# Moving the low halves of some weight blocks from VectorE to GpSimd, and splitting every u block of the selection stage

## The chip, the cores and the metric

The kernel runs on one core of a Trainium2 chip. The metric is the device time in microseconds (us) of one launch. Before the change three runs gave 1626.18, 1627.36 and 1630.89 us, median 1627.36 us.

## The reference, cut to what matters

The reference is a two-layer decoder trunk on 272 tokens (16 meta tokens and 256 sequence tokens) of width 1024, all in float32. Each layer has a token mixing part (projections, a gated recurrence, attention) and a PEER part, which is a retrieval over 16384 one-neuron experts:

```
q = (h @ wq)                      # 8 heads, two halves of 128
s = einsum(q, subkeys)            # 128 scores per half
top 16 of each half, 16 best of their 256 sums -> experts, gates (softmax)
act = gelu(h . u[expert])         # one number per token and expert
out = sum over experts of gate * act * v[expert]
```

The result is added to `h`. Both layers read 16384 x 1024 float32 numbers of `u` and as many of `v`.

## The kernel before, in words

For most tokens (208 of 256) the kernel does not gather experts. It multiplies the normalised tokens with all of `u`, in 128 blocks of 128 experts, applies gelu, multiplies with a dense matrix of gates that is zero where an expert was not selected, and multiplies with all of `v`. The other 48 tokens (and the 16 meta tokens in the first layer) take a sparse way: their rows of `u` and `v` are gathered by indirect DMAs that GpSimd issues, and VectorE does the sums.

A float32 weight block of 128 x 1024 is loaded by a DMA of SyncE into a buffer (`raw`, seven of them; later also free parts of `act` and `gtab`). To multiply at float16 speed with enough precision it is split in two float16 halves in `conv` (lines 221 to 240): ScalarE writes `hi`, the block times 1024 rounded to float16 (line 238), and VectorE writes `lo`, the block times 1024 minus `hi` (line 239). TensorE then does 24 matmuls for a block in `mm3` (lines 259 to 268): eight chunks of `hi` with the high part and with the low part of the tokens (lines 264 and 265), and then eight chunks of `lo` with the high part (line 268). There are three buffers of `hi` and three of `lo` (`NHL`), and a block is split two blocks ahead of the one that TensorE is about to multiply.

The table `WHOLE` names pairs of blocks that are not split. TensorE multiplies those in float32, with eight matmuls for a block that the records show as 16 (line 1148 for `u`, 1191 for `v`), and ScalarE and VectorE do nothing for them. In the first layer the pairs 1, 5, 9, 13 and 17 of `u` (blocks 2, 3, 10, 11, and so on up to 35) are whole, in the second layer the pairs 1, 3, 6, 10 and 14 (blocks 2, 3, 6, 7, 12, 13, 20, 21, 28, 29).

The selection runs beside this. In the query stage TensorE multiplies 16 blocks of `wq` (lines 1117 to 1131). From each head's scores VectorE takes the top 16 (`topk16`, lines 785 to 792). Then `select_idx` (lines 794 to 842) forms the experts and gates for 128 tokens at a time. In it ScalarE makes a widened copy (line 820) that needs a cast by VectorE (line 805), and an exponential (line 834), which needs a table load before it and another before the next gelu. This work is cut in steps by a generator. After each `wq` and each `u` block `pump` lets the next steps be issued until a budget is used up (line 1162: about 1.15 for a u block, plus 1.6 for an unsplit one). So the table of numbers sets how much selection work stands between two blocks in the program; a scheduler then orders the instructions of each engine, and the splitting has raised priority. All engines work in order: an instruction that waits holds up all that stands behind it on its engine.

When the second half of the tokens is selected, 24 small DMAs on GpSimd's queue (line 950) rearrange the experts and gates of the sparse tokens. After that, in steps of eight tokens, one-hot matrices are built and multiplied to the dense gates (lines 982 to 1010), up to about block 110. The gathers of the sparse tokens begin at block 56 (first layer) or 54.

Of the kernel before, what the change touches and what calls it, by code (L numbers as in the profile page):

```python
# [15 lines left out]
AF = mybir.ActivationFunctionType  # L16
ALU = mybir.AluOpType
# [29 lines left out]
WS = 1024.0  # L47
# [2 lines left out]
UB = (((56, 126, 28),), ((54, 127, 20),))  # L50
PF = 7
XV = 6
WHOLE = {"uT": ((1, 5, 9, 13, 17), (1, 3, 6, 10, 14)), "v": ((15, 24, 33, 42, 51, 60), ())}
NHL = 3
ATT = ((3, 7), (1, 7))
LRU_AT = (1, 2, 3, 4)
LRU_FIRST = 0
# [2 lines left out]
VEND = 127.0  # L60
NWARM = 48
NC2 = 112


def whole(w, l, b):
# [84 lines left out]
def trunk(tc, a, out, dbg=None):  # L150
    nc = tc.nc
    V, A, P, G = nc.vector, nc.scalar, nc.tensor, nc.gpsimd
# [13 lines left out]
    with ExitStack() as ctx:  # L166
# [15 lines left out]
        order = []  # L182
# [38 lines left out]
        def conv(n):  # L221
            while st["conv"] < min(n, len(order)):
                k = st["conv"]
                issue(len(order))
                f = raws.pop(k)
                r = f[2]
                st["conv"] += 1
                if whole(*order[k]):
                    hls[k] = (k,) + f[1:]
                    continue  # L230
                free.append((k,) + f[1:])
                if order[k][0] == "gather":
                    hook["step"](r, *order[k][2])
                    continue
                hi = hl_p.tile([128, D], F16, name="hi", tag="hi")
                lo = hl_p.tile([128, D], F16, name="lo", tag="lo")
                with tc.high_priority(offset=PRI):
                    A.activation(hi, r, AF.Copy, scale=WS)  # L238
                    V.scalar_tensor_tensor(out=lo, in0=r, scalar=WS, in1=hi, op0=ALU.mult, op1=ALU.subtract)  # L239
                hls[k] = (hi, lo)  # L240

        def ahead(k, n):
# [600 lines left out]
        def peer(l, col, hh, hl, rs, wq0):  # L843
            with tc.tile_pool(name="peer", bufs=1) as pp:
# [118 lines left out]
                prog = {"u": 0, "t": 0, "b": PUMP[1]}  # L963
# [148 lines left out]
                for h in range(8):  # L1112
                    qh = qT[:, h % 2]
                    for q in range(2):
                        if h == 0 and q == 0:
                            o = wq0
                        else:
                            w = block("wq", l, 2 * h + q)
# [21 lines left out]
                for j in range(NK):  # L1140
                    w = block("uT", l, j)
                    if j % 2 == 0:
                        o2 = ps("u")
                    oj = o2[:, (j % 2) * SD:(j % 2) * SD + SD]
                    raw = whole("uT", l, j)
                    if raw:
                        for c in range(8):
                            P.matmul(oj, w[2][:, c * 128:c * 128 + 128], xn[:, c], start=j % 2 == 0 and c == 0, stop=c == 7, skip_group_check=True)  # L1148
                        free.append(w)
                    else:  # L1150
                        mm3(oj, w, xh, xlo, first=j % 2 == 0)
                    if j % 2:
                        td = prog["t"]
                        assert not (raw and td)
                        ov = o2[:, 0:2 * SD].rearrange("p (j t) -> p j t", j=2)
                        if td < SD:
                            A.activation(act[:, j - 1:j + 1, td:SD], ov[:, :, td:SD], AF.Gelu, scale=1.0 if raw else 1.0 / WS)  # L1157
                        if td:
                            A.activation(gt2[:, :, 0:td], ov[:, :, 0:td], AF.Gelu, scale=1.0 / WS)
                            V.tensor_tensor(out=act[:, j - 1:j + 1, 0:td], in0=act[:, j - 1:j + 1, 0:td], in1=gt2[:, :, 0:td], op=ALU.mult)  # L1160
                        prog["u"] = j + 1
                    pump(prog["b"] - prog["t"] / 960.0 + (1.6 if raw else 0.0))
                drain()
                pv = [ps("v") for _ in range(4)]
                ww = area("hn", F16, [128, 4, 2, 2, SD], "ww")
# [13 lines left out]
                for j in range(NK):  # L1179
                    w = block("v", l, j)  # L1180
# [13 lines left out]
                    hi, lo = w  # L1194
# [70 lines left out]
```

## Time and profile before

| | us |
|---|---|
| runs, median of three | 1627.36 (1626.18 to 1630.89) |
| profiled execution | 1629.76 |
| its span, first to last instruction | 1627.9 |
| TensorE busy in the span | 1562.6 (96%) |
| VectorE | 1489.6 (92%) |
| ScalarE | 1062.8 (65%) |
| GpSimd | 408.2 (25%) |

A busy share is a mean over stages: mixing of the first layer (about 0 to 147 us), its query stage (147 to 198), u blocks (198 to 531), v blocks (to 835), then the same for the second layer with its first u block at 1016.6 us. Matmuls overlap, so a record of 0.25 us is not the time that a matmul takes of TensorE; the distance of two starts is. The same holds for the other engines: the next record starts some 0.1 us before the last one ends.

### The profile page before, as it was taken

The page shows a single profiled execution, that of the slowest core. Times are in us where ns is not written, and L with a number is a line of the kernel's source. Part 1 is how long each engine was busy: PE and PEld are TensorE (multiplying, and loading weights), DVE is VectorE, ACT ScalarE, POOL GpSimd, SP SyncE. Part 2 cuts the span into 40 slices and gives each one's busy share as a digit, 9 for nine tenths or more (in the row PEclk, how much of TensorE's full clock was granted, in tenths as well). Part 3 has the DMA queues.
Part 4 walks back from the last instruction along what each step waited for, and adds up shares of the span by engine and source line. Part 5 has one row for each costly group of instructions (what it writes and reads, how often), then busy time and mean ns, then how long its engine had stood idle before and what let it go on. Part 6 is the DMA issues. An engine that isn't in the chain of part 4 may idle for free.

```text
span 1627.9 us, 39712 instructions
## 1 busy us (share of the span) xinstructions
PE 1562.6 (96%) x15662; PEld 1459.8 (90%) x15662; DVE 1489.6 (92%) x3088; ACT 1062.8 (65%) x1984; POOL 408.2 (25%) x296
## 2 busy tenths in 40 slices
PE   8999989989999999999999899899999999999998
PEld 6757888989989999999977678799999999999998
DVE  6988989889999999889988889997899989999997
ACT  6857555798786645555457666467998756555653
POOL 1000000311213686465410000002111123655441
PEclk9999999999999999999999999999999999999999
DMA  8304465668879999999973143467678789999993
GB/s 311 117 1 163 142 205 195 230 204 276 287 263 343 396 408 408 408 388 408 408 284 107 37 146 131 168 213 241 215 269 289 266 312 390 407 407 399 381 393 147
DMA packets 122571, 437.98 MB, mean 269 GB/s; under 512 B 15184, under 2 KB 16592, under 8 KB 121872
## 3 DMA queue, kind: packets, MB, share of 16 engines
q1 hardware_dynamic: 88592, 317.88, 53.5%
q0 software_dynamic: 33792, 117.56, 19.4%
q8 instruction: 123, 2.02, 0.5%
q14 instruction: 64, 0.52, 0.1%
HBM read 434.24 MB, written 1.05 MB: 267 GB/s over the span
## 4 chain that ended last, share of the span: by engine, by line
PE 50%; DVE 9%; issue 5%; ACT 2%; POOL 1%; DMA 1%; DVEq 0%; POOLq 0%; ACTq 0%; SPq 0%
PE ps_v L1199 32%; PE ps_u L264 3%; PE ps_u L265 3%; PE ps_u L268 3%; DVE lo L239 3%; PE ps_v L1191 2%; PE ps_g L1060 1%; PE ps_v L998 1%; DVE act L791 1%; DVE act L788 1%; PE ps_u L1148 1%; ACT hi L238 1%; PE ps_v L264 1%; PE ps_v L265 1%; POOL raw L1099 1%
## 5 line engine op out<-in xcount | busy, mean ns | idle before, releaser
L238 ACT ACTIVATE hi<-raw 128x1024 f16<-128x1024 f32 x380 | 399.8, 1058 | 196.5 <-PE ps_v L1199 77.6
L239 DVE SCALAR_TENSOR_TENSOR lo<-raw,hi 128x1024 f16<-128x1024 f32 x380 | 464.5, 1225 | 55.3 <-ACT hi L238 51.6
L264 PE MATMUL ps_u<-hn,hi 128*128 128x208 f16 (+2 forms) x1952 | 374.1, 255 | 25.2 <-ACT act L1157 12.7
L1199 PE MATMUL ps_v<-ww,hi 128*128 128x208 f16 x3904 | 393.4, 254 | 2.8 <-ACT ww L1172 1.7
L265 PE MATMUL ps_u<-hn,hi 128*128 128x208 f16 (+2 forms) x1952 | 374.2, 255 | 0.0
L1199 PEld LDWEIGHTS <-hi 128*128 128x128 f16 x3904 | 353.2, 99 | 4.8 <-issue 3.5
L265 PEld LDWEIGHTS <-hi 128*128 128x128 f16 x2496 | 245.7, 98 | 33.6 <-issue 21.6
L264 PEld LDWEIGHTS <-hi 128*128 128x128 f16 x2496 | 245.8, 98 | 27.5 <-ACT hi L238 9.5
L238 ACT ACTIVATE hi<-act 128x1024 f16<-128x1024 f32 x157 | 166.1, 1058 | 125.1 <-PE ps_v L1199 90.9
L268 PEld LDWEIGHTS <-lo 128*128 128x128 f16 x2496 | 229.6, 98 | 16.5 <-DVE lo L239 5.7
L268 PE MATMUL ps_u<-hn,lo 128*128 128x208 f16 (+2 forms) x1952 | 219.4, 255 | 3.1 <-DVE lo L239 3.0
L1199 PE MATMUL ps_v<-ww,lo 128*128 128x208 f16 x1952 | 217.0, 253 | 0.1
L239 DVE SCALAR_TENSOR_TENSOR lo<-act,hi 128x1024 f16<-128x1024 f32 x157 | 191.7, 1223 | 21.8 <-ACT hi L238 19.2
L1099 POOL DMA_INDIRECT raw<-ur,act x72 | 100.1, 1390 | 330.1 <-DVE lo L239 168.3
L1199 PEld LDWEIGHTS <-lo 128*128 128x128 f16 x1952 | 176.4, 98 | 1.2 <-DVE lo L239 1.0
L950 POOL DMA_DIRECT2D act<-act x48 | 24.4, 518 | 561.3 <-PE ps_v L954 294.9
L989 ACT ACTIVATE ohb<-oha,gtab 128x128 f16<-128x128 f16 x416 | 134.3, 406 | 4.5 <-DVE oha L984 2.4
L1099 POOL DMA_INDIRECT raw<-v,act x57 | 103.4, 1814 | 81.6 <-DVE acc L1086 39.2
L264 PE MATMUL ps_v<-hgx,hi 128*128 128x272 f16 (+1 forms) x480 | 113.8, 277 | 0.5 <-DVE hT L1240 0.4
L265 PE MATMUL ps_v<-hgx,hi 128*128 128x272 f16 (+1 forms) x480 | 113.6, 277 | 0.2 <-DVE hgx L333 0.2
L1099 POOL DMA_INDIRECT act<-v,act x48 | 91.7, 1911 | 70.2 <-DVE acc L1086 32.5
L1099 POOL DMA_INDIRECT act<-ur,act x38 | 60.7, 1598 | 112.9 <-DVE lo L239 43.7
(327 smaller groups left out, 2275.8 us busy)
## 6 DMA issues: line engine op xcount, KB each, us to landing
raw<-uT SPq DMA_DIRECT2D x220, 512.0 KB
act<-v SPq DMA_DIRECT2D x126, 512.0 KB
raw<-v SPq DMA_DIRECT2D x111, 512.0 KB
act<-uT SPq DMA_DIRECT2D x36, 512.0 KB
raw<-wq SPq DMA_DIRECT2D x32, 512.0 KB
raw<-w_in SPq DMA_DIRECT2D x28, 512.0 KB
gtab<-v SPq DMA_DIRECT2D x19, 512.0 KB
raw<-w_out SPq DMA_DIRECT2D x16, 512.0 KB
```

The source lines that it names most:

```text
L238: A.activation(hi, r, AF.Copy, scale=WS)
L239: V.scalar_tensor_tensor(out=lo, in0=r, scalar=WS, in1=hi, op0=ALU.mult, op1=ALU.subtract)
L264: P.matmul(o, hi[:, s], xhi[:, c], start=first and c == 0, stop=False, skip_group_check=True)
L265: P.matmul(o, hi[:, s], xlo[:, c], start=False, stop=False, skip_group_check=True)
L268: P.matmul(o, lo[:, s], xhi[:, c], start=False, stop=c == n - 1, skip_group_check=True)
L788: V.match_replace(out=w, in_to_replace=tv[:, 0:8], in_values=src, imm_value=-3.0e38)
L791: V.max_index(out=ti[:, 8:16], in_max=tv[:, 8:16], in_values=w)
L950: G.dma_start(out=egs[h * 16:h * 16 + 16, g], in_=comb[p:p + 16, :, h * 16:h * 16 + 16])
L989: A.activation(ob[:, 1, t], oe[:, t], AF.Copy, scale=gl[:, b * 8 + t:b * 8 + t + 1])
L1099: G.indirect_dma_start(out=t, out_offset=None, in_=tab, in_offset=bass.IndirectOffsetOnAxis(ap=ei[g][:, s:s + 1], axis=0))
L1191: P.matmul(o, w[2][:, c * 128:c * 128 + 128], act[:, j], start=False, stop=False, skip_group_check=True)
L1199: P.matmul(o, (hi, hi, lo)[k][:, s], (wh, wl, wh)[k], start=j == 0 and k == 0 and c % 2 == 0, stop=j == NK - 1 and k == 2, skip_group_chec ...
```

## The change

Three things change. No `u` pair is unsplit any more. Every second `wq` block (odd ones) and every second `u` block (even ones, below block 40 in the first layer and below 34 in the second) is "pooled": ScalarE first multiplies the raw block by 1024 in place, then writes `hi` from it, and GpSimd subtracts to get `lo`, where VectorE did it before. And the extra budget for the selection steps is 1.15 for each pooled `u` block where it was 1.6 for each unsplit one. 53 blocks are pooled: 8 and 20 in the first layer, 8 and 17 in the second.

```
-WHOLE = {"uT": ((1, 5, 9, 13, 17), (1, 3, 6, 10, 14)), "v": ((15, 24, 33, 42, 51, 60), ())}
+WHOLE = {"uT": ((), ()), "v": ((15, 24, 33, 42, 51, 60), ())}
+LOW_POOL = (40, 34)
+def pooled(w, l, b):
+    return w == "wq" and b % 2 == 1 or w == "uT" and b % 2 == 0 and b < LOW_POOL[l]
...
-                    A.activation(hi, r, AF.Copy, scale=WS)
-                    V.scalar_tensor_tensor(out=lo, in0=r, scalar=WS, in1=hi, op0=ALU.mult, op1=ALU.subtract)
+                    if pooled(*order[k]):
+                        A.activation(r, r, AF.Copy, scale=WS)
+                        A.activation(hi, r, AF.Copy)
+                        G.tensor_tensor(out=lo, in0=r, in1=hi, op=ALU.subtract)
+                    else:
+                        A.activation(hi, r, AF.Copy, scale=WS)
+                        V.scalar_tensor_tensor(out=lo, in0=r, scalar=WS, in1=hi, op0=ALU.mult, op1=ALU.subtract)
...
-                    pump(prog["b"] - prog["t"] / 960.0 + (1.6 if raw else 0.0))
+                    pump(prog["b"] - prog["t"] / 960.0 + (1.15 if pooled("uT", l, j - 1) else 0.0))
```

Lines below 50 of the kernel stay, later ones move down by one to ten (line 238 becomes 248 for a block that is not pooled; a pooled block has 244, 245 and 246).

GpSimd's queue in the first layer, from its last small instruction of the mixing part to the first gathers, before:

```order
L443 MEMSET kx 32x2x272
L443 MEMSET qx 32x2x272
L370 TENSOR_TENSOR lw<-eb,lw 128x4
L950 DMA act<-act 16x2x16 x24
L1099 DMA act<-ur,act 128x1024
L1099 DMA raw_73<-ur,act 128x1024
```

And now, from the last pooled blocks on (the numbers are those of the raw buffers; the last `lo` is that of block 38):

```order
L246 TENSOR_TENSOR lo<-raw_72,hi 128x1024
L246 TENSOR_TENSOR lo<-raw_67,hi 128x1024
L246 TENSOR_TENSOR lo<-raw_69,hi 128x1024
L246 TENSOR_TENSOR lo<-raw_71,hi 128x1024
L960 DMA act<-act 16x2x16 x24
L246 TENSOR_TENSOR lo<-raw_73,hi 128x1024
L1109 DMA raw_68<-ur,act 128x1024
```

27 subtractions now stand ahead of the 24 small DMAs, and the 28th stands behind them. In the second layer the same DMAs stand in groups of 7, 8 and 9 with one subtraction after the first group and one after the second.

ScalarE's queue at one place of the first layer's u blocks where it makes a widened copy for the selection, before:

```order
L834 ACT_TABLE_LOAD
L834 ACTIVATE act<-act 128x128
L1157 ACT_TABLE_LOAD
L1157 ACTIVATE act<-ps_u 128x416
L238 ACTIVATE hi<-raw_72 128x1024
L820 ACTIVATE act<-act 128x2048
L238 ACTIVATE hi<-raw_67 128x1024
L238 ACTIVATE hi<-raw_68 128x1024
L1157 ACTIVATE act<-ps_u 128x416
```

And now a stretch with the same table loads (`raw<-raw` is the scaling in place, 248 and 245 are the `hi` of blocks that are not pooled and that are):

```order
L248 ACTIVATE hi<-raw_68 128x1024
L244 ACTIVATE raw_73<-raw_73 128x1024
L844 ACT_TABLE_LOAD
L844 ACTIVATE act<-act 128x128
L245 ACTIVATE hi<-raw_69 128x1024
L1167 ACT_TABLE_LOAD
L1167 ACTIVATE act<-ps_u 128x416
L248 ACTIVATE hi<-raw_70 128x1024
L245 ACTIVATE hi<-raw_71 128x1024
L1167 ACTIVATE act<-ps_u 128x416
```

For a pair of blocks ScalarE now has two `hi`, one scaling and one gelu, where an unsplit pair had only the gelu. The selection steps stand among them as before.

## Rows read from the trace of the kernel before

**Rows 1.** The page, busy time of each engine in the whole span.
```profile
PE 1562.6 (96%) x15662; PEld 1459.8 (90%) x15662; DVE 1489.6 (92%) x3088; ACT 1062.8 (65%) x1984; POOL 408.2 (25%) x296
```

**Rows 2.** Stretches: length, busy PE, PEld, DVE, ACT, POOL, granted clock, DMA.
```profile
147.00:198.00 51.00, 50.46 (x423) 41.73 (x422) 49.17 (x227) 33.14 (x80) 0.00 (x0) 1.00 0.45 148
...
198.20:301.20 103.00, 94.93 (x875) 92.19 (x873) 97.64 (x363) 59.23 (x80) 0.00 (x0) 0.98 0.58 195
1018.80:1112.30 93.50, 82.77 (x732) 80.94 (x730) 86.51 (x307) 51.06 (x73) 12.15 (x24) 0.95 0.59 198
```

**Rows 3.** Timeline of TensorE: start, length; starts of u blocks in both layers.
```profile
198.71 0.25 PE L264 MATMUL ps_u<-hn,hi 128*128 128x208 f16 x1
...
200.85 5.81 PE L1148 MATMUL ps_u<-act,raw 128*128 128x208 f32 x32
206.50 0.25 PE L264 MATMUL ps_u<-hn,hi 128*128 128x208 f16 x1
...
207.93 0.88 PE L268 MATMUL ps_u<-hn,lo 128*128 128x208 f16 x8
208.64 0.25 PE L264 MATMUL ps_u<-hn,hi 128*128 128x208 f16 x1
...
301.15 0.25 PE L264 MATMUL ps_u<-hn,hi 128*128 128x208 f16 x1
...
1019.72 0.25 PE L264 MATMUL ps_u<-hn,hi 128*128 128x208 f16 x1
...
1112.25 0.25 PE L264 MATMUL ps_u<-hn,hi 128*128 128x208 f16 x1
```

**Rows 4.** Waits of TensorE, us in total, times, longest: 198 to 301, 1018 to 1112.
```profile
PE ps_u L264 <- ACT hi L238: 4.4, 1, 4.4
...
PE ps_u L264 <- ACT act L1157: 10.7, 2, 7.6
```

**Rows 5.** Waits of ScalarE for VectorE: 198 to 301, then 1018 to 1112.
```profile
ACT act L820 <- DVE act L805: 14.3, 3, 7.3
ACT act L834 <- DVE act L833: 6.7, 1, 6.7
...
ACT act L820 <- DVE act L805: 13.2, 2, 9.7
ACT act L820 <- DVE act L823: 2.1, 1, 2.1
```

**Rows 6.** Timeline of ScalarE around two `hi` back to back.
```profile
258.38 1.99 ACT L238 ACTIVATE hi<-raw 128x1024 f16<-128x1024 f32 x2
260.27 0.49 ACT L1157 ACTIVATE act<-ps_u 128x416 f32<-128x416 f32 x1
```

**Rows 7.** Timeline of VectorE around one `lo`.
```profile
145.23 1.22 DVE L239 SCALAR_TENSOR_TENSOR lo<-raw,hi 128x1024 f16<-128x1024 f32 x1
146.37 0.43 DVE L313 TENSOR_TENSOR Pm<-Pm 128x272 f32<-128x272 f32 x1
```

**Rows 8.** Timeline of GpSimd, two of its instructions at the start.
```profile
2.00 0.55 POOL L443 MEMSET qx<- 32x544 f32 x1
...
5.81 1.08 POOL L370 TENSOR_TENSOR lw<-eb,lw 128x4 f32<-128x4 f32 x1
```

**Rows 9.** Groups by line, VectorE 198 to 291; VectorE and GpSimd 560 to 600.
```profile
L239 DVE SCALAR_TENSOR_TENSOR lo<-raw,hi 128x1024 f16<-128x1024 f32 x27 | 33.0, 1232 | 4.8 <-ACT hi L238 4.8
...
L239 DVE SCALAR_TENSOR_TENSOR lo<-act,hi 128x1024 f16<-128x1024 f32 x9 | 10.9, 1219 | 1.2 <-issue 0.8 <-ACT hi L238 0.4
...
L1099 POOL DMA_INDIRECT raw<-v,act x9 | 22.4, 2492 | 2.7 <-issue 2.4 <-DMA raw<-v,act 0.3
```

**Rows 10.** Timeline of VectorE and GpSimd around the 24 small DMAs, first layer.
```profile
300.67 0.28 DVE L944 SCALAR_TENSOR_TENSOR act<-act 128x128 int32<-128x128 f32 x1
...
301.82 4.28 POOL L950 DMA_DIRECT2D act<-act  x8 [294.94 <-PE ps_v L954]
...
317.04 0.51 POOL L950 DMA_DIRECT2D act<-act  x1 [0.39 <-DMA act<-act]
```

## The prediction

> **What bounds the kernel now.** I read the page's busy times first, then the stretches of the two selection stages, then who waits in them, then single instructions. TensorE is busy 96% of the span and VectorE 92% [rows 1], so a gain can only come from where TensorE is held up or does dearer work than it must. The change touches only the query stage and the first 40 (34) u blocks, so I look at these. In the query stage of the first layer TensorE is busy 50.46 of 51 us and VectorE 49.17, ScalarE only 33.14 [rows 2]: TensorE sets the pace and VectorE just follows. In the u blocks VectorE is the busiest, 97.64 of 103 us in the first layer and 86.51 of 93.5 in the second, TensorE less, ScalarE little over half [rows 2].
>
> How much could go at most? A split u block takes 2.14 us of TensorE (206.50 to 208.64). An unsplit pair takes 5.65 us (200.85 to 206.50) against 4.28 for a split pair [rows 3]. From block 1 to block 40 of the first layer (198.71 to 301.15, counted on TensorE's timeline) 102.4 us pass; 39 blocks at 2.14 are 83.5, so 19.0 us are spare. From block 1 to block 34 of the second (1019.72 to 1112.25) it is 92.5 us against 33 x 2.14 = 70.6, so 21.9 [rows 3]. Of these 40.9 us the unsplit blocks are 20 x 0.69 = 13.7 (5.65 less 4.28, halved, for each block). The rest is TensorE waiting, most of it for ScalarE: 4.4 us for one `hi`, 10.7 us in two waits for a gelu that had to free its PSUM bank [rows 4], and the slower clock behind these gaps (granted 0.98 and 0.95 on the mean of the stretches [rows 2]). And ScalarE in those places waits for VectorE: 14.3 and 6.7 us in the first layer, 13.2 and 2.1 in the second [rows 5]. The chain is: VectorE is late with a selection step, ScalarE stands in order before the copy or the exponential that needs it, the `hi` and gelu behind it come late, TensorE starves.
>
> **The change part by part.** *Unsplit pairs go.* TensorE gains the 13.7 us. ScalarE and VectorE get the splitting of these blocks back.
>
> *VectorE.* In the first layer 8 query blocks and 20 u blocks leave VectorE and 10 u blocks come back: 18 `lo` less. In the second, 8 + 17 - 10 = 15 less. One takes 1.14 us of VectorE from start to start [rows 7]: 20.5 and 17.1 us, 37.6 together. 8 x 1.14 = 9.1 of it in each layer falls in the query stage, where it shortens nothing by itself, but VectorE then enters the u blocks that much less late.
>
> *ScalarE.* Two `hi` in a row take 1.89 us (258.38 to 260.27), 0.945 each [rows 6]; I price the scaling in place, which reads and writes float32, the same, since the trace shows none (bounds: nothing, where ScalarE would wait anyway, and twice 0.945, should a float32 write go at half the rate). First layer: 10 `hi` come back and 20 scalings are added, 30 x 0.945 = 28.4 us on 59.2 [rows 2]: 87.6 us, which is more than TensorE's 83.5. Second: 10 + 17 = 27, 25.5 us on 51.1: 76.6, more than 70.6. So ScalarE becomes the engine that sets the least time of the stage: at best 102.4 - 87.6 = 14.8 and 92.5 - 76.6 = 15.9 us are gained, 30.7 together, not 40.9. In the query stage eight scalings (7.6 us) lie in the 17.9 us that ScalarE has free there.
>
> *GpSimd.* The trace shows no subtraction of this size. From below: one pass over 1024 elements at the rate of a memset (0.55 us for 544 [rows 8]) is 1.0 us. From above: three passes (two reads, a write) and the 1.08 us that a tensor_tensor of four elements takes [rows 8], 4.2. I take the middle, 2.6. That is hidden as long as `lo` comes in time: the buffer of a block's `hi` is free when TensorE ends the `hi` part three blocks before, and `lo` is needed one `lo` part (0.71, from 207.93 to 208.64), two blocks (4.28) and one `hi` part (1.43) later [rows 3], 6.4 us; less 1.05 for `hi` itself (1.99 less 0.945 [rows 6]) that leaves 5.3 us for 2.6. GpSimd is idle there before (0.00 in the first two stretches [rows 2]). The cover is gone when something else stands ahead in its queue (below).
>
> *What GpSimd takes from VectorE.* Nearest row: a `lo` of VectorE lasts 1.219 us while GpSimd is busy with gathers, 1.232 with GpSimd idle [rows 9], so no cost; but those are DMA issues, not arithmetic. From above: VectorE stands for the whole 2.6. I take 0.25 us for each, near the row: 7.0 and 6.3 us. Then VectorE is relieved by 13.5 and 10.8 us net, and ScalarE's waits for it shrink from 21.0 to 7.5 and from 15.3 to 4.5. The stages take 87.6 + 7.5 = 95.1 and 76.6 + 4.5 = 81.1: gains of 7.3 and 11.4 us.
>
> *The queue behind the small DMAs.* The `lo` of block 38 now stands behind 24 DMAs on GpSimd. They start about a microsecond after VectorE's index instruction (300.67 and 301.82) and last until 317.55 [rows 10], 16.9 us after it, of which TensorE passes some six blocks and two one-hot steps. In the new order that instruction stands between the `lo` of blocks 35 and 37, so TensorE is at about block 34 or 35. It then comes to the low part of block 38 some 8 to 10 us later, and has to wait for the DMAs and the subtraction. Bounds: 0, if VectorE is earlier than I think or the waiting is made good by engines that were behind, and 9 us. I take 5. In the second layer the DMAs are cut in groups with the subtractions between, at most nine in a row, some 4.5 us: I take nothing.
>
> *The rest* (later u blocks, v blocks, mixing) does the same matmuls and loads. The selection ends a few blocks earlier, so some gate products are done on fewer rows and eight more pairs take the two-step gelu; both are on engines that TensorE does not wait for there.
>
> The sum: -7.3 - 11.4 + 5 = -13.7 us. On the profiled execution's 1629.8 us that is 1616.1; the median of the runs is 2.4 us lower than the profiled one, so 1613.7. I say 1614.
>
> **Rivals.** *All waits go* and nothing collides; the DMAs do no harm. Then ScalarE's floor holds, -30.7: 1599.1, or 1597 on the scale of the median. For it: the relief of VectorE (20.5 and 17.1) is as large as ScalarE's waits (21.0 and 15.3). Against: ScalarE has no slack left, so each remaining wait is paid in full.
>
> *VectorE and GpSimd hold each other up* (slower). Both read two operands from SBUF for the same kind of work. In the first layer's window VectorE spends at least a third of its time in such instructions (33.0 us on `lo` alone [rows 9]). If each of the 53 subtractions costs VectorE 1.0 us, 53 us are lost against 37.6 won, VectorE stays the bound and the time is 15.4 us longer: 1645, or 1643 on the median's scale. It decides from 37.6 / 53 = 0.71 us each. For it: a GpSimd instruction of 2.6 us is longer than two of VectorE's. Against: the `lo` beside busy GpSimd of [rows 9]. The Trainium skill, page "SBUF — State Buffer", section "Who interferes with whom", says that a VectorE instruction with two SBUF inputs and a GpSimd instruction that reads SBUF exclude each other for the whole instruction, whichever starts second waiting. By that rule this rival is the likelier; no row here has GpSimd arithmetic beside VectorE, so the trace neither bears it out nor refutes it.
>
> *ScalarE keeps waiting* and eats the gain. Half of the waits stay (10.5 and 7.7 us): stages of 98.1 and 84.3, -4.3 - 8.2, and the DMAs cost their 9: -3.5, 1626.3, or 1624 on the median's scale. For it: the copies of line 820 wait for the end of a fixed row of top-16 instructions, however early VectorE starts. Against: these waits grew from a VectorE that was never idle.
>
> **How the numbers follow.** A difference of 0.3% (4.9 us) is about what a measurement of this kernel can tell from none: faster is below 1622.5, slower above 1632.2. I give my forecast 0.42 (its own range 1606 to 1623), "all waits go" 0.2, "ScalarE keeps waiting" 0.18, "hold each other up" 0.2. Faster is 0.2 and 0.4 of the 0.42, that is 0.6; same 0.2; slower 0.2. The range from 1595 to 1638 takes in the second case whole and of the slow case the part up to some 0.9 us for each subtraction.
>
> **What would show it.** Right: no matmuls of line 1148's kind; TensorE's starts of u blocks 2.14 us apart nearly everywhere; ScalarE busy over 85% in the two stretches; block 40 within 97 us of block 1 in the first layer and block 34 within 83 in the second; waits of ScalarE for VectorE below 8 us in each; one wait of TensorE for a `lo` from GpSimd near block 38, about 5 us. Wrong: a `lo` of VectorE that lasts 2 us or more where a subtraction runs, or subtractions of 4 us and more; TensorE waiting for GpSimd at many blocks; VectorE still without idle time to block 40.

## The result, and the profile after

The changed kernel takes 1668.26 us (median of four runs, 1666.32 to 1671.38) against 1627.21 for the kernel before on the same chip: 1.0252 of it, 95% interval [1.0232, 1.0272]. It is 41 us slower; the forecast was 1614 with a range up to 1638.

Where the 41 us lie can be read from TensorE's starts: the last block of `w_out` ends the mixing part, the first u block ends the query stage, the last u block ends the u stage. Lengths in us (L0 and L1 are the first and the second layer), each from one profiled execution, so that 2 or 3 us of a difference mean little:

| | query, L0 | u blocks, L0 | between | query, L1 | u blocks, L1 |
|---|---|---|---|---|---|
| before | 56.6 | 333.4 | 432.5 | 55.1 | 322.3 |
| changed | 65.2 | 351.7 | 434.8 | 66.7 | 325.2 |

Both query stages lose (8.6 and 11.6 us), where nothing was expected to change, and the u blocks of the first layer lose 18.

The page after: the busy line, and the two new groups (busy us, mean ns of one, idle time before them and what ended most of it).

```profile
PE 1564.6 (94%) x15822; PEld 1452.6 (87%) x15822; DVE 1510.2 (90%) x3059; ACT 1131.1 (68%) x2053; POOL 527.8 (32%) x349
...
L246 POOL TENSOR_TENSOR lo<-raw,hi 128x1024 f16<-128x1024 f32 x53 | 124.8, 2358 | 459.5 <-ACT hi L245 399.2
...
L244 ACT ACTIVATE raw<-raw 128x1024 f32<-128x1024 f32 x53 | 55.6, 1052 | 58.7 <-DMA raw<-uT 52.4
```

Against [rows 1], VectorE's busy time has risen by 20.6 us although 33 `lo` have left it; ScalarE is up by 68. The last row is the new thing: ScalarE stood still for 58.7 us ahead of the scalings, nearly all of it for loads of u.

The stretches from block 1 to block 40 of the first layer and over the first 34 blocks of the second, the columns as in [rows 2], and TensorE's starts as in [rows 3]:

```profile
205.70:337.30 131.60, 99.63 (x994) 91.97 (x992) 107.00 (x308) 91.91 (x129) 57.47 (x42) 0.92 0.48 166
1055.30:1153.10 97.80, 82.83 (x847) 77.70 (x847) 93.81 (x264) 75.15 (x101) 50.14 (x39) 0.95 0.54 185
```

```profile
205.68 0.25 PE L274 MATMUL ps_u<-hn,hi 128*128 128x208 f16 x1
...
322.78 0.25 PE L274 MATMUL ps_u<-hn,hi 128*128 128x208 f16 x1
331.77 1.57 PE L278 MATMUL ps_u<-hn,lo 128*128 128x208 f16 x8 [8.74 <-POOL lo L246]
...
337.26 0.25 PE L275 MATMUL ps_u<-hn,hi 128*128 128x208 f16 x1
...
1058.88 0.25 PE L274 MATMUL ps_u<-hn,hi 128*128 128x208 f16 x1
...
1153.06 0.25 PE L274 MATMUL ps_u<-hn,hi 128*128 128x208 f16 x1
```

Block 1 to block 40 now takes 131.6 us (205.7 to 337.3), where it took 102.4, and block 1 to block 34 of the second layer 94.2, where it took 92.5. No engine is full: VectorE is busy 107.0 of 131.6 us, ScalarE 91.9. Engines that all have spare time while the stretch is 29% longer are waiting for each other. In the middle stands the stop of TensorE for block 38's `lo`, 8.74 us. GpSimd's timeline shows why, beside [rows 10]: that `lo` starts when the last small DMA is issued. By the end of the u stage 11 of the 29 us lost up to block 40 are made good (351.7 against 333.4).

```profile
314.34 4.26 POOL L960 DMA_DIRECT2D act<-act  x8 [3.78 <-ACT ohb L999]
...
322.62 6.94 POOL L960 DMA_DIRECT2D act<-act  x14 [0.89 <-DMA act<-act]
329.58 2.13 POOL L246 TENSOR_TENSOR lo<-raw,hi 128x1024 f16<-128x1024 f32 x1
```

ScalarE's waits (us in total, times, longest) from 203 to 330, from 1056 to 1150, and one of the kernel before, from 1018 to 1112, beside [rows 5]:

```profile
ACT raw L244 <- DMA raw<-uT: 20.0, 8, 6.4
ACT act L830 <- DVE act L815: 4.6, 2, 2.5
...
ACT act L955 <- DVE act L849: 3.8, 1, 3.8
ACT hi L245 <- DVE lo L249: 1.7, 1, 1.7
ACT act L830 <- DVE act L833: 1.6, 1, 1.6
...
ACT raw L244 <- DMA raw<-uT: 16.2, 10, 3.8
ACT act L830 <- DVE act L815: 2.0, 1, 2.0
ACT act L830 <- DVE act L833: 1.2, 1, 1.2
...
ACT hi L238 <- DMA raw<-uT: 6.8, 1, 6.8
```

The waits for VectorE's selection steps are as small as was hoped: 6.2 us (4.6 and 1.6) where [rows 5] has 21.0, and 3.2 where it has 15.3. With two waits of other kinds it is 11.7 us in the first layer. Waits for loads have taken their place, where before ScalarE waited for a load of u once, 6.8 us, in all the query and early u blocks of both layers.

Two things can be seen at work in the trace. The first is a ring, here in the query stage of the second layer (timeline of GpSimd, SyncE and ScalarE put in order of time: start, length, and idle time before with what ended it):

```profile
1032.05 2.13 POOL L246 TENSOR_TENSOR lo<-raw,hi 128x1024 f16<-128x1024 f32 x1 [5.71 <-ACT hi L245]
...
1034.21 0.33 SPq L160 DMA_DIRECT2D raw<-uT  x1
...
1037.34 1.06 ACT L244 ACTIVATE raw<-raw 128x1024 f32<-128x1024 f32 x1 [1.65 <-DMA raw<-uT]
1038.30 1.04 ACT L245 ACTIVATE hi<-raw 128x1024 f16<-128x1024 f32 x1
...
1039.42 2.13 POOL L246 TENSOR_TENSOR lo<-raw,hi 128x1024 f16<-128x1024 f32 x1 [5.24 <-ACT hi L245]
...
1041.58 0.33 SPq L160 DMA_DIRECT2D raw<-uT  x1
...
1044.79 1.06 ACT L244 ACTIVATE raw<-raw 128x1024 f32<-128x1024 f32 x1 [2.09 <-DMA raw<-uT]
```

The subtraction ends at 1034.18 and frees a `raw` buffer; 0.03 us later SyncE issues the next load; 3.13 us after that a scaling starts that waited for this very load (it waits for the semaphore that the load sets); the `hi` of an earlier block follows, then the next subtraction, and its end lets the next load go. One round is 7.37 us (1032.05 to 1039.42) for two query blocks; before, the last heads of this stage, each with its two blocks, came every 6.4. The scaling needs nothing but the load and has raised priority, and the scheduler put it on ScalarE mostly (40 of 53 times) ahead of four or five `hi` of other blocks: in the order of ScalarE's queue shown with the change, `raw_73` is scaled ahead of the `hi` of 69, 70 and 71. ScalarE works in order and stands there for a load that has just been issued: here the seven buffers give no lead any more.

The second is that GpSimd and VectorE hold each other up (VectorE and GpSimd, first layer):

```profile
254.78 2.15 POOL L246 TENSOR_TENSOR lo<-raw,hi 128x1024 f16<-128x1024 f32 x1 [7.60 <-ACT hi L245]
...
254.99 0.26 DVE L797 FIND_INDEX8 act<-act 128x8 uint32<-128x112 f32 x1
...
255.96 1.52 DVE L809 TENSOR_TENSOR act<-act 128x512 f32<-128x512 f32 x1
...
259.64 7.35 POOL L246 TENSOR_TENSOR lo<-raw,hi 128x1024 f16<-128x1024 f32 x2 [2.72 <-ACT hi L245]
...
259.93 1.21 DVE L831 TENSOR_TENSOR act<-act,iok 128x2048 f16<-128x2048 f16 x1
...
262.59 2.41 DVE L837 TENSOR_TENSOR act<-act 128x1024 f16<-128x1024 f16 x1
...
265.04 2.23 DVE L837 TENSOR_TENSOR act<-act 128x512 f16<-128x512 f16 x1
```

The two subtractions from 259.64 last 7.35 us where two alone take 4.3, and the two products of line 837 beside them last 2.41 and 2.23. The search beside the first subtraction, which reads one operand, keeps its 0.26; the product of line 831, with two, keeps its 1.21 as well, and there it is the subtraction that lasts longer (4.81 for the first of the two). So the two do hold each other up; which one pays depends on where each stands. The means of the same products and of `lo` in this stretch (203 to 300; the last two rows are those of the kernel before, 198 to 291):

```profile
L249 DVE SCALAR_TENSOR_TENSOR lo<-raw,hi 128x1024 f16<-128x1024 f32 x15 | 20.6, 1376 | 7.6 <-ACT hi L248 7.6
L833 DVE TENSOR_TENSOR act<-act 128x2048 f16<-128x2048 f16 x3 | 7.3, 2417 | 0.0
...
L837 DVE TENSOR_TENSOR act<-act 128x1024 f16<-128x1024 f16 x3 | 3.8, 1256 | 0.0
```

```profile
L823 DVE TENSOR_TENSOR act<-act 128x2048 f16<-128x2048 f16 x3 | 3.7, 1234 | 0.0
L827 DVE TENSOR_TENSOR act<-act 128x1024 f16<-128x1024 f16 x3 | 2.1, 699 | 0.0
```

What this costs VectorE in all can be read from three pages of runs below: e6 (the changed kernel without subtractions and scalings, and with exactly as many instructions on VectorE), e1 (the changed kernel with `hi` ahead of the scaling), and e7 (e1 with the subtractions on VectorE itself):

```profile
PE 1544.5 (96%) x15822; PEld 1443.6 (90%) x15822; DVE 1456.8 (91%) x3059; ACT 1080.9 (67%) x2000; POOL 407.4 (25%) x296
PE 1551.5 (94%) x15822; PEld 1446.6 (88%) x15822; DVE 1498.6 (91%) x3059; ACT 1131.2 (69%) x2053; POOL 517.5 (31%) x349
PE 1553.1 (95%) x15822; PEld 1445.5 (88%) x15822; DVE 1511.9 (92%) x3112; ACT 1131.6 (69%) x2053; POOL 405.8 (25%) x296
```

With the same 3059 instructions VectorE is busy 53.4 us longer in the changed kernel than in e6 (1510.2 less 1456.8), 1.01 us for each of the 53 subtractions; in e1 it is 41.8 us, 0.79 each. A subtraction done by VectorE itself costs 1.04 (e7, 55.1 us). So moving them has hardly relieved VectorE: by 1.7 us in the changed kernel, by 13.3 with the order of e1.

### The profile page after: what moved, and what is told of

Read it like the earlier page. It is cut to its first block, busy times and chain, and to the rows that moved or that the text cites. A ratio compares the mean times of both kernels' runs of the same rounds, so it can differ in the third digit from the quotient of the medians.

```text
span 1669.6 us, 40142 instructions
## 1 busy us (share of the span) xinstructions
PE 1564.6 (94%) x15822; PEld 1452.6 (87%) x15822; DVE 1510.2 (90%) x3059; ACT 1131.1 (68%) x2053; POOL 527.8 (32%) x349
## 3 DMA queue, kind: packets, MB, share of 16 engines
HBM read 434.24 MB, written 1.05 MB: 261 GB/s over the span
## 4 chain that ended last, share of the span: by engine, by line
PE 51%; DVE 9%; ACT 4%; issue 1%; DMA 1%; POOL 0%; DVEq 0%; ACTq 0%
PE ps_v L1209 29%; PE ps_u L274 4%; PE ps_u L275 4%; PE ps_u L278 4%; DVE lo L249 2%; PE ps_v L1201 2%; ACT hi L248 1%; PE ps_v L1008 1%; PE ps_v L274 1%; PE ps_v L275 1%; PE ps_v L278 1%; PE ps_g L1070 1%; DMA act<-v 1%; DVE acc L1096 0%; PE ps_g L309 0%
## 5 line engine op out<-in xcount | busy, mean ns | idle before, releaser
L249 DVE SCALAR_TENSOR_TENSOR lo<-raw,hi 128x1024 f16<-128x1024 f32 x350 | 432.1, 1238 | 67.8 <-ACT hi L248 55.9
L248 ACT ACTIVATE hi<-raw 128x1024 f16<-128x1024 f32 x350 | 368.2, 1055 | 176.6 <-PE ps_v L1209 89.4
L274 PE MATMUL ps_u<-hn,hi 128*128 128x208 f16 (+1 forms) x2112 | 407.9, 256 | 17.8 <-ACT act L1167 6.9
L275 PE MATMUL ps_u<-hn,hi 128*128 128x208 f16 (+1 forms) x2112 | 407.6, 256 | 0.0
L1209 PEld LDWEIGHTS <-hi 128*128 128x128 f16 x3904 | 353.7, 99 | 5.0 <-issue 3.5
L278 PEld LDWEIGHTS <-lo 128*128 128x128 f16 x2656 | 244.6, 99 | 59.5 <-DVE lo L249 29.5
L274 PEld LDWEIGHTS <-hi 128*128 128x128 f16 x2656 | 263.4, 99 | 31.2 <-issue 8.2
L275 PEld LDWEIGHTS <-hi 128*128 128x128 f16 x2656 | 263.1, 99 | 26.8 <-issue 14.7
L278 PE MATMUL ps_u<-hn,lo 128*128 128x208 f16 (+1 forms) x2112 | 240.5, 257 | 38.4 <-DVE lo L249 24.1
L246 POOL TENSOR_TENSOR lo<-raw,hi 128x1024 f16<-128x1024 f32 x53 | 124.8, 2358 | 459.5 <-ACT hi L245 399.2
L1209 PEld LDWEIGHTS <-lo 128*128 128x128 f16 x1952 | 176.9, 98 | 1.4 <-DVE lo L249 1.0
L1109 POOL DMA_INDIRECT act<-v,act x50 | 99.0, 1980 | 75.9 <-DVE acc L1096 32.8
L1109 POOL DMA_INDIRECT raw<-v,act x55 | 94.5, 1718 | 81.6 <-DVE acc L1096 40.9
L244 ACT ACTIVATE raw<-raw 128x1024 f32<-128x1024 f32 x53 | 55.6, 1052 | 58.7 <-DMA raw<-uT 52.4
```

What stands on the lines that cost most here:

```text
L244: A.activation(r, r, AF.Copy, scale=WS)
L246: G.tensor_tensor(out=lo, in0=r, in1=hi, op=ALU.subtract)
L274: P.matmul(o, hi[:, s], xhi[:, c], start=first and c == 0, stop=False, skip_group_check=True)
L275: P.matmul(o, hi[:, s], xlo[:, c], start=False, stop=False, skip_group_check=True)
L278: P.matmul(o, lo[:, s], xhi[:, c], start=False, stop=c == n - 1, skip_group_check=True)
L1109: G.indirect_dma_start(out=t, out_offset=None, in_=tab, in_offset=bass.IndirectOffsetOnAxis(ap=ei[g][:, s:s + 1], axis=0))
```

## The experiments

Three theories at the start. **A**: the scaling that stands ahead on ScalarE waits for loads (the ring). **B**: VectorE and GpSimd hold each other up. **C**: ScalarE simply has too much work. Fifteen kernels ran, on four chips, each beside the kernel before; r is the ratio to it on the same chip, with its 95% interval, and differences between runs are taken from r. Stage lengths are again from one profile each:

| | query, L0 | u blocks, L0 | between | query, L1 | u blocks, L1 | r |
|---|---|---|---|---|---|---|
| e1 | 59.1 | 343.6 | 432.9 | 56.9 | 328.5 | 1.0102 |
| e2 | 58.2 | 341.7 | 432.4 | 59.8 | 328.9 | 1.0089 |
| e3 | 56.6 | 337.3 | 429.4 | 54.9 | 330.4 | 1.0040 |
| e4 | 63.3 | 326.6 | 430.0 | 62.4 | 316.5 | 1.0009 |
| e5 | 59.2 | 327.5 | 432.7 | 56.9 | 318.2 | 0.9969 |
| e6 | 57.7 | 325.8 | 429.6 | 55.0 | 310.2 | 0.9881 |
| e7 | 56.8 | 340.5 | 431.6 | 54.4 | 330.6 | 1.0087 |
| e9 | 59.2 | 331.7 | 434.5 | 56.9 | 321.1 | 0.9998 |
| e11 | 59.1 | 324.9 | 431.2 | 56.9 | 318.9 | 0.9928 |
| e13 | 59.1 | 341.5 | 430.0 | 57.2 | 326.5 | 1.0114 |
| e15 | 64.9 | 339.5 | 433.7 | 64.2 | 318.5 | 1.0140 |

### e1: the high half first

```
-  A.activation(r, r, AF.Copy, scale=WS)
-  A.activation(hi, r, AF.Copy)
+  A.activation(hi, r, AF.Copy, scale=WS)
+  A.activation(r, r, AF.Copy, scale=WS)
```

> One edit on the changed kernel: for a pooled block ScalarE writes hi first (scaling as it reads) and scales the raw block in place behind it, so that the scaling cannot stand ahead of the block's own hi. Theory A (order on ScalarE): in the changed kernel the in-place scalings stand 2 to 6 hi ahead of their own block in ScalarE's queue and wait there for a load that is just being issued; ScalarE's waits of the scaling for loads (7.9 + 20.0 us in the first layer, 8.3 + 16.2 in the second) go to under 5 us in all, the query stages go back from 65 and 67 us to 55 to 58, the time falls by 25 to 50 us, to 1618 to 1643. Theory B (VectorE and GpSimd hold each other up): nothing of that changes, the time stays within 8 us of 1668. Theory C (ScalarE simply has too much work): the same 53 extra instructions, the time stays within 8 us of 1668, ScalarE's waits turn into other waits.

Measured: 1647.37 us, 1.0102 [1.006, 1.0145]. The same instructions in another order are 1.50% (24 us) faster than the changed kernel, though not quite down to A's range; B and C had both put it within 8 us of 1668. Both query stages come back to 59.1 and 56.9. ScalarE no longer shows a wait for a load of u; the scaling now directly follows its `hi` (timeline of ScalarE, second layer's query stage):

```profile
1022.51 1.06 ACT L244 ACTIVATE hi<-raw 128x1024 f16<-128x1024 f32 x1 [0.39 <-issue]
1023.47 0.37 ACT L1131 ACTIVATE act<-ps_v 128x256 f32<-128x256 f32 x1
1023.73 1.05 ACT L245 ACTIVATE raw<-raw 128x1024 f32<-128x1024 f32 x1
```

Mending the order takes away more than half of the loss, as A said. 17 us are left.

### e2: the subtraction on VectorE, scaling ahead as in the changed kernel

```
-  G.tensor_tensor(out=lo, in0=r, in1=hi, op=ALU.subtract)
+  V.tensor_tensor(out=lo, in0=r, in1=hi, op=ALU.subtract)
```

> One edit on the changed kernel: the subtraction of pooled blocks goes to VectorE (tensor_tensor, same operands); the in-place scalings stay where they are and GpSimd has no arithmetic. Theory A: the scalings still wait for loads (over 25 us in all), and the time is at least 15 us longer than the kernel that only drops the unsplit pairs (e3). Theory B: no collisions any more, VectorE's 2048-element products of the selection go back from 1.95 to about 0.86 us, and the time is within 8 us of e3. Theory C: as A in time, but with ScalarE busy over 85% of the u stretch and waits for loads under 10 us.

Measured: 1644.59 us, 1.0089 [1.0062, 1.0116]. That is 0.49% (8 us) over e3: A's 15 us and more are missed, B's 8 us just met, and the products are back (line 833 in this run: a mean of 0.85 us, 1.95 in the changed kernel over the same shapes). But A's sign is there too, and nearly as large as in the changed kernel (27.9 and 24.5 us there): ScalarE waits for loads, here from 137 to 330 and from 972 to 1145:

```profile
ACT raw L244 <- DMA raw<-uT: 25.0, 14, 4.1
...
ACT raw L244 <- DMA raw<-uT: 19.3, 11, 2.8
```

So the waits alone are not what costs.

### e7: the subtraction on VectorE and the high half first

Both edits together.

> The changed kernel with the high half first, the scaling behind it, and the subtraction on VectorE: no GpSimd. Against the run with the high half first on GpSimd (1647.4) it changes the engine of the subtraction alone, against the kernel without unsplit pairs (1636.9) it adds the 53 scalings alone. If ScalarE's extra work is hidden and GpSimd is dearer than VectorE itself (collisions, the 24 DMAs ahead): 1635 to 1641. If ScalarE's extra 50 us is what costs (theory C): 1645 to 1655. If GpSimd's relief of VectorE is worth something: above 1650.

Measured: 1640.42 us, 1.0087 [1.0067, 1.0107], in the first of the three ranges; C's is missed. With e1, e2 and the changed kernel this is a square, the order of scaling and `hi` against the engine of the subtraction:

| r | scaling ahead | scaling behind |
|---|---|---|
| GpSimd | 1.0252 | 1.0102 |
| VectorE | 1.0089 | 1.0087 |

The order costs 24 us with GpSimd and nothing measurable with VectorE, and the engine costs 27 us with the scaling ahead (e2) and nothing measurable with it behind. So neither A nor B is right alone: it takes both together. In the query stages, where 16 of the 24 us lie (e1 against the changed kernel), the trace shows how: the ring. In the u blocks it is less clear, for there the order also changes the collisions: of the 24 us of time some part is the 11.6 us by which VectorE is busier in the changed kernel than in e1 (1510.2 against 1498.6). No run separates the two. And with the order mended, GpSimd in place of VectorE is worth nothing (1.0102 against 1.0087, the intervals overlap). VectorE's busy time shows why: of 55.1 us of subtractions that it no longer does, 41.8 come back as waiting for GpSimd's.

### e3: no unsplit pairs, no pooling; e12: the same with the old budget

e3 is the changed kernel with `pooled` always false and the extra 1.15 where the changed kernel has it. e12 gives the extra 1.6 to the formerly unsplit blocks instead, so that nothing differs from the kernel before but the 20 blocks being split.

> The changed kernel without pooling: no unsplit u pairs, every low half on VectorE, no in-place scaling, the same extra budget of selection steps for every second u block. All theories: TensorE saves 13.7 us, VectorE gets 20 low halves (22.8 us) back and was already the busiest engine, so the time is 5 to 15 us over the kernel before: 1632 to 1645. It is the floor against which e2 is read. Should it be under 1627, VectorE was not the bound in the selection stage.

> The kernel before with the 20 unsplit u blocks split and nothing else: no pooling, the budget 1.6 at the same blocks as before. Theory V (the low halves given back to VectorE eat what TensorE gains): 1632 to 1640, as with the new budget (1.0040 of before). Rival (the new table of budgets, 1.15 at 20 and 17 blocks, made that loss): 1614 to 1627.

Measured: e3 1636.90 us, 1.0040 [1.0022, 1.0057], as expected; e12 1632.45, 1.0015 [0.9997, 1.0033]. Splitting the pairs is worth at best nothing, where TensorE's 13.7 us had been expected; the new budget costs about 0.25% more (4 us, hardly clear of the noise). On the scale of 1627 us e12's interval is 1627 to 1633, between the two ranges: the budget was probably part of e3's loss, but without it there is still no gain.

### e8: the formerly unsplit blocks without a low half; e6: the pooled blocks without one

e8 is e3, and e6 the changed kernel, in which the named blocks set `lo = hi`: no low half is made, and TensorE does the same number of matmuls.

> No unsplit u pairs and no pooling (as the run at 1636.9), but the 20 blocks that were unsplit before get no low half: TensorE multiplies with the high half twice. TensorE's work as in that run, VectorE's 20 x 1.14 = 23 us less. Theory V (the low halves given back to VectorE eat TensorE's 13.7 us and more): 1614 to 1624. Rival (the order of the selection or TensorE's clock sets the stage, the unsplit pairs saved VectorE nothing that counts): 1632 to 1638.

> The changed kernel, where the 53 pooled blocks have no low half at all: no scaling, no GpSimd subtraction, nothing on VectorE; TensorE multiplies with the high half twice. It shows what the relief of VectorE is worth if it costs nothing. Theory V (VectorE's backlog sets the length of the two selection stages): with 53 x 1.14 = 60 us less than the kernel without unsplit pairs (1636.9) at the rate seen with the query blocks alone (5.9 us of u blocks for 9.1 us of VectorE): 1590 to 1610. Rival (the fixed chain of the selection and ScalarE's order set it): 1622 to 1637.

Measured: e8 1627.06 us, 0.9989 [0.9973, 1.0005]; e6 1607.15, 0.9881 [0.9862, 0.99]. VectorE's backlog does set the stages: 23 us of `lo` taken from it give 8.3 us of time (0.51%), 60 us give 26 (1.59% against e3). That is 0.36 to 0.43 us for one of VectorE, less than theory V's range for e8 (1614 to 1624), while e6 lies in its range. e6 bounds what any way of pooling these blocks could bring: 26 us against e3, 19 against the kernel before, if scaling and subtraction cost nothing. With VectorE relieved it is no longer full (e6, first 40 and 34 blocks; columns as in [rows 2]):

```profile
195.00:293.40 98.40, 90.84 (x1010) 88.57 (x1009) 86.28 (x326) 73.03 (x104) 10.12 (x20) 1.00 0.64 222
1017.40:1101.60 84.20, 78.66 (x865) 76.01 (x864) 74.40 (x230) 66.93 (x108) 12.08 (x24) 0.98 0.66 229
```

### e4: the query blocks alone; e5: the same with the high half first

The kernel before, unsplit pairs kept, with only the 16 odd `wq` blocks pooled; e5 has the order of e1.

> The kernel before with only the odd query blocks pooled (16 in all) and the unsplit u pairs and their budget kept. Theory A: the query stages take about 65 us where they took 56 and 55 (the ring of load, scaling, hi, subtraction, buffer), VectorE enters the u blocks less late; 1627 + 20 less up to 15: 1632 to 1647. Theory B: 16 collisions of about half a microsecond against 18 us of relief: 1610 to 1627. Theory C: ScalarE has room in the query stage, so as B.

> The kernel before with only the 16 odd query weight blocks pooled, the high half written first and the scaling behind it; unsplit u pairs as before. Ring theory (a scaling that stands ahead waits for a load, and the load for GpSimd): query stages of about 59 and 57 us as with the high half first in the changed kernel (63.3 and 62.4 with the scaling ahead, 56.6 and 55.1 before), u blocks 5 to 6 us shorter in each layer as with the scaling ahead: 1619 to 1627 us. Collision theory (the subtractions cost VectorE as much as they save): query stages stay above 61 us, 1628 to 1636.

Measured: e4 1630.91 us, 1.0009 [0.9988, 1.003]; e5 1622.15, 0.9969 [0.9957, 0.9982]. In e4 the query stages grow by 6.7 and 7.3 us and the u blocks shrink by 6.8 and 5.8: VectorE's relief (9.1 us in each layer) comes out later, as the prediction said, and the ring takes it away in the query stage. e5 removes most of the ring (59.2 and 56.9) and keeps the relief. The numbers for e4 were missed on both sides: A had left the relief out, B and C the ring. e5 lies in the ring theory's range.

### e10: GpSimd's low halves made, but not read

e1 with `lo = hi` behind the subtraction.

> High half first; GpSimd makes the 53 low halves, but TensorE multiplies with the high half twice, so nothing on TensorE waits for GpSimd; the raw buffers still do. Without any subtraction and scaling it was 1607, and the 53 scalings cost 3.5 to 8 us (1636.9 to 1640.4, or by the ratios 0.47%). Collision theory (about 0.5 us of VectorE for each, 26 us, worth 0.43 us of time for one of VectorE as the low halves were): 1622 to 1632. Lateness theory (what costs is that TensorE waits for a low half of GpSimd, the small DMAs among it): 1611 to 1618.

Measured: 1652.16 us, 1.0145 [1.0122, 1.0168], above both ranges. That TensorE waits for low halves of GpSimd is thus not what makes pooling dear: here it waits for none of them and the time is no better than e1's. TensorE waits for those of VectorE instead (waits from 195 to 330, e10's row first, then e1's two; and e10's `lo` on VectorE, 203 to 300):

```profile
PE ps_u L279 <- DVE lo L250: 17.0, 10, 4.4
```

```profile
PE ps_u L278 <- DVE lo L249: 9.1, 5, 4.1
PE ps_u L278 <- POOL lo L246: 9.0, 6, 1.8
```

```profile
L250 DVE SCALAR_TENSOR_TENSOR lo<-raw,hi 128x1024 f16<-128x1024 f32 x16 | 26.1, 1634 | 5.6 <-ACT hi L249 5.6
```

A `lo` of VectorE has a mean of 1.63 us where [rows 9] has 1.232. The direction is that of the collision theory, the size (2.64% or 43 us over e6, of which the scalings are 8) is more than it forecast: it had 0.5 us of VectorE for each subtraction, and VectorE's busy time is 48.8 us above e6's (1505.6 against 1456.8), 0.92 each. That is also more than in e1 (0.79), which fits a time that is not below e1's; why the subtractions collide more here stays open.

### e9, e13, e14: the last pooled blocks

All with the high half first. e9: `LOW_POOL = (30, 26)`, nine blocks fewer, and the extra budget goes with them. e14: the same blocks, but the budget of (40, 34). e13: `LOW_POOL = (38, 30)` with the budget of (40, 34); only the three subtractions behind or among the 24 small DMAs are gone.

> As the run with the high half first (1647.4), but only u blocks below 30 (26) are pooled, so that no subtraction stands behind or among the 24 small DMAs: 44 subtractions, not 53. Theory Q (the queue behind the small DMAs costs the 5 to 9 us it shows in TensorE's row): 1634 to 1641. Rival (TensorE's stop there is made good later, as VectorE is late anyway): 1643 to 1649.

> As the run with the high half first (1.0102 of before), but the three subtractions that stand behind or among the 24 small DMAs on GpSimd (block 38 of the first layer, 30 and 32 of the second) go back to VectorE; the budgets stay those of blocks below 40 and 34. Theory Q (what the last nine pooled blocks cost is that queue): most of the 17 us comes back, 1.000 to 1.004 of before, 1627 to 1635. Rival P (each late subtraction costs by itself, by colliding with the one-hot steps and products): a third of it, 1.005 to 1.009, 1637 to 1644. Rival B (it was the budget): as it was, 1.008 to 1.012.

> High half first, pooled below 30 and 26 only (as the run at 0.9998), but the extra budget of 1.15 stays for blocks below 40 and 34. It separates the two things that run changed. Rival B (the smaller budget gave the 17 us): near 1.006 to 1.012 of before. Theories Q and P (the nine subtractions cost it): 0.998 to 1.003.

Measured: e9 1628.86 us, 0.9998 [0.9984, 1.0011]; e13 1645.89, 1.0114 [1.0088, 1.0141]; e14 1634.94, 1.0049 [1.0033, 1.0065]. Without its last nine pooled blocks the kernel is 17 us faster than e1, more than either theory of e9 had said. The queue behind the small DMAs has no part in it that can be seen (e13 is where e1 is, to within some 8 us): from block 38 to block 39 of the first layer e1 takes 13.6 us and e13 3.1, and block 40 comes 123.4 us after block 1 in e1, 111.6 in e13; but of these 11.8 us 9.6 are lost again from block 40 to the last (217.1 and 226.7). Six pooled blocks that are not behind the DMAs cost 0.65% (11 us, e13 to e14), and the budget 0.51% (8 us, e14 to e9). Theory Q falls; P and B each hold for a part, e14 lying between their ranges. By P the late blocks are dearer than the early ones because they lie beside VectorE's wide products; that was seen (below), not tested.

### e15: the changed kernel with fewer blocks

The changed kernel with `LOW_POOL = (30, 26)`, scaling ahead.

> The changed kernel as it is (scaling ahead of its high half), but pooled only below 30 and 26. With the high half first that was worth 17 us. If ring and late blocks are two separate costs: 1.0252 less 0.0104, 1.012 to 1.018 of before, 1648 to 1657. If the ring's 24 us sit in the last nine blocks themselves: 0.999 to 1.006. If the ring covers the late blocks (they come in time because all is late): 1.020 to 1.026.

Measured: 1650.39 us, 1.0140 [1.0108, 1.0171]. Against e9 the early scaling costs 1.42% (23 us), as it did between the changed kernel and e1 (24): it is a cost of its own and adds to the rest. 13 of the 23 us lie in the query stages.

### e11: query blocks and 13 u blocks, unsplit pairs kept

e5, and every fourth u block that is not unsplit, below 30 and 26, pooled as well.

```
+    return w == "wq" and b % 2 == 1 or w == "uT" and b % 4 == 0 and b < LOW_POOL[l] and not whole(w, l, b)
```

> High half first, 16 query blocks pooled, unsplit u pairs kept (as the run at 0.9969 of before), and 13 u blocks pooled as well: every fourth that is not unsplit, below 30 and 26. If a subtraction on GpSimd beside the u blocks still relieves VectorE (1.14 less some 0.5 us, half of it seen in the time): 0.993 to 0.996 of before, 1616 to 1621. Rival (in the u blocks it gives back what it takes, as between the run on GpSimd at 1.0102 and the run on VectorE at 1.0087): 0.996 to 1.000.

Measured: 1617.34 us, 0.9928 [0.991, 0.9946]. It beats the kernel before by 0.72% (12 us) and the changed kernel by some 50 us: pooling pays where the order is mended, the pairs stay unsplit, and the subtractions are few and early. Which of the last two counts for more was not separated. VectorE is busy 16.7 us less than in the kernel before (1472.9 against 1489.6), where 29 `lo` at 1.14 are 33: half of the relief is kept.

## Why the prediction was wrong, step by step

One path from the kernel before to the changed one, in per cent of 1627 us (differences of ratios, each known to some 0.2 to 0.5; on another path, by way of e2, the 1.50 would fall to the subtraction on GpSimd, since it takes both): pairs split +0.15 (e12), new budget +0.25 (e3), 53 scalings +0.47 (e7), the subtraction on GpSimd +0.15 (e1), the scaling ahead of its high half +1.50: 2.52, or 41 us.

- *ScalarE's scaling.* This step failed most. Its price of 0.945 us was right (records of 1.05, starts 0.96 apart). But it was priced as work alone, in the query stage in ScalarE's free time, without asking where it stands. The order of the queue, shown with the change, had it ahead of other blocks' `hi`, and what it waits for there is a load. Together with the subtraction on GpSimd that is 24 of the 41 us.
- *The stage as 87.6 + 7.5.* ScalarE was to become the bound, over 85% busy. It was busy 91.91 of 131.6 us (70%) and 75.15 of 97.8 (77%).
- *Unsplit pairs, 13.7 us.* TensorE's work did shrink, but TensorE was not what the stage waited for: the `lo` of these blocks goes to the engine that was the busiest. e12 is +0.15% [-0.03, +0.33], not -0.8%; taking these low halves away again (e8) gives 8.3 us.
- *VectorE's relief, 37.6 us.* Counted rightly, valued too high. e6 shows 0.43 us of time for one of VectorE, and that when nothing is paid for it. What is paid is the next term.
- *Collisions, 0.25 us each.* This is the other step that failed, mis-sized by a factor of three to four: 1.01 us in the changed kernel, 0.79 in e1 (VectorE's busy time against e6). Both are above the 0.71 from which the rival was to decide, so the net relief of 13.5 and 10.8 us was not there. Counted instruction by instruction (each beside a subtraction against the same line and shape alone) it comes to some 50 us in the changed kernel: about 0.5 for each subtraction in the query stages, 1.0 and 1.3 in the u blocks. The rival "hold each other up", with 1.0 us each, was right in this mechanism; that its 1643 lies near e1's 1647 is in part luck, since the path above is made of other terms. The prediction's own signs for it came: a `lo` of 3.14 us, and subtractions of 4.41 and 4.81. The row on which I relied, `lo` beside busy GpSimd in [rows 9], was beside DMA issues, which is another thing than arithmetic. The Trainium skill's page "SBUF — State Buffer", "Who interferes with whom", by which two-operand work of VectorE and a GpSimd instruction that reads SBUF exclude each other, had it right against that row. The trace agrees: a product of line 839 that starts 0.09 us after a subtraction ends 0.15 us after it, and takes 2.19 us where it takes 0.28 alone (GpSimd and VectorE, second layer):

```profile
1087.05 2.13 POOL L246 TENSOR_TENSOR lo<-raw,hi 128x1024 f16<-128x1024 f32 x1 [4.05 <-PE ps_u L278]
1087.14 2.19 DVE L839 TENSOR_TENSOR act<-act 128x128 f32<-128x128 f16 x1
```

- *GpSimd's subtraction, 2.6 us.* 2.13 alone, 2.36 in the mean, within the bounds; the two longest, 4.41 and 4.81, are above them.
- *The queue behind the small DMAs, 5 us (0 to 9).* The wait came where it was forecast and took 8.74 us. Its cost in the end is near nothing as far as the runs can tell (e13 against e1, where TensorE stands at the same block): the 0 of the bounds, "made good by engines that were behind".
- *ScalarE's waits for VectorE.* Right for the copies and the exponentials: 6.2 and 3.2 us, below 8 in each layer (11.7 in the first with the two waits of other kinds). It shows that the chain named as the bound was broken, and that the next one was not seen.

## What to carry to other kernels

An instruction that depends only on a load and has raised priority may be put far ahead by the scheduler, and on an engine that works in order everything behind it then waits for that load. Before moving the last reader of a load buffer to a slower engine, follow the buffer round: reader, release, issue, landing, first user; if the first user stands ahead of work that the reader needs, the prefetch is gone. And an engine relieved is worth only what remains after the helper has held it up, and only for as long as that engine is the bound.

## What the runs showed of the hardware that was not expected

- Which instructions of VectorE suffer beside a GpSimd subtraction is nearly all or nothing. In the query and u stages of the changed kernel, `lo` (two operands) took 1.21 us in the mean alone and 1.68 beside one (14 of them, the longest 3.14), line 901 (two operands) 0.48 and 1.41, the products of line 837 a median of 0.68 and 2.41 at 1024 wide and of 0.42 and 2.15 at 512; the search and replace instructions of the top 16 (one wide operand) took the same 0.27 alone and beside one, in some 40 pairs each. One operand is not always enough to be spared: two casts of line 815 took 0.79 and 1.00 beside a subtraction and 0.28 alone. Two subtractions also took 7.35 us instead of 4.3 beside wide products. Of the nine subtractions around each query stage of the changed kernel the first four each cost VectorE 1.2 to 1.9 us, beside products with two operands, and the last five, beside the search, nothing. So the query stage, where most of VectorE's work is of that kind, is the cheap place for arithmetic on GpSimd.
- After the stop of 8.74 us the granted clock of TensorE was at the lower of its two levels (1.2 of 2.4 GHz) for a while, and back soon after (length, busy engines, clock of 333 to 337 and 337 to 345):

```profile
333.00:337.00 4.00, 4.00 (x25) 3.49 (x24) 2.65 (x4) 2.12 (x6) 0.00 (x0) 0.50 0.97 369
337.00:345.00 8.00, 8.00 (x102) 7.98 (x101) 6.83 (x11) 7.97 (x22) 0.00 (x0) 0.99 0.64 214
```
